# Slot weights of a mixture-of-experts layer: from one-hot matmuls to a gather from DRAM

## The chip, the cores and the metric

The kernel runs on one core of a Trainium2 chip. The metric is the device time of one execution in microseconds (us); lower is better. The core has a matrix engine (PE, with PEld for its weight loads), a vector engine (DVE), a scalar engine (ACT), GpSimd (POOL) and a sync engine (SP). Each engine takes its own instructions strictly in the order in which they were written for it; an instruction that waits holds up all that stand behind it on that engine. PE writes only into PSUM banks; DVE and ACT read them out. SP issues the loads of weights, POOL the indirect transfers (gather and scatter by row number).

## The reference, cut to what matters

One encoder layer on 512 tokens of width 1024: gated attention beside a spatial gating unit, a cross-attention, and a mixture of 16 experts, of which each token uses two. All inputs are float32. The part that the change is about:

```python
def hierarchical_moe(h, w_rg, b_rg, w_re, b_re, w_gate, w_up, w_down):
    t = h.reshape(B * S, D)                                   # 512 x 1024
    gprob = softmax(t @ w_rg + b_rg)                          # 4 groups
    gval, gidx = top_k(gprob, 1)
    elog_sel = (t @ w_re + b_re).reshape(-1, 4, 4)[group gidx]
    evals, eidx = top_k(elog_sel, 2)
    ew = softmax(evals) * gval
    expert_id = gidx * 4 + eidx
    combine = sum(one_hot(expert_id, 16) * ew[..., None])     # 512 x 16
    for e in range(16):
        he = silu(t @ w_gate[e]) * (t @ w_up[e])              # 1024 -> 512
        y = y + combine[:, e:e + 1] * (he @ w_down[e])        # 512 -> 1024
```

## The kernel before, in words

The first 455 us or so hold the attention parts and the router. Then 16 experts follow one another; that stage takes the rest of the span and is what the change touches.

**Slots.** For every expert the kernel gathers the tokens that chose it into 128 slots, so that one PE pass serves the expert. `oh_e(e)` builds on DVE a one-hot matrix (token by slot) from the positions `posm`. `ids_e(e)` multiplies it on PE with a small table `vals` (four matmuls, one for each 128 tokens), so that a PSUM bank holds, slot by slot, the row number of the token in `h3d` (the normed tokens in DRAM) and its row in the output buffer `ybuf`; DVE turns them into integers in `ixall`. `gather` is an indirect DMA from `h3d` into `xes[e % 2]`, `xtr` transposes that tile on PE (eight transposes into `pt_xt`, two banks) and splits it into a high and a low part.

**Slot weights, before.** `vals` has five columns: two for the numbers and three for the combine weight, cut into three float16 pieces by `weight_tables` on POOL (9 instructions for the weights, 8 more for the pieces). `slot_weights` puts the three pieces together on DVE in four small instructions (`sw`, then a column of `wsl`). For experts 0 to 3 (`NLATE`) the numbers are wanted before the weights are known; for these `late(e)` builds the one-hot again, runs `weight_of` (four more matmuls into a bank, `wt_e`, and the four DVE instructions), then scales the finished output `ye[e]` on ACT and scatters it. From expert 4 on, ACT scales while it reads the output out of PSUM.

**Weights of the experts.** Each expert has six chunks of 1 MB: 0 and 1 gate, 2 and 3 up, 4 and 5 down. A chunk is two halves. A half is split for fp32 accuracy: ACT rounds it into `h_e` (L128), DVE subtracts to get `l_e` (L129, a "low"). The fourth field of `W.order` names the halves whose low goes to POOL instead: in the experts 1 to 14, one of the twelve halves, the first of chunk 1 (`POOLJ`). PE runs six matmuls for each half: h with h, l with h, h with l (L237 to L239).

**Order.** `expert_period(e)` is one round: eight halves of gate and up of expert e, with a table `hooks[j, i]` of things to do after half i of chunk j, then `fin` (silu times up), `xtr` of expert e+1, and `down_scatter(e - 1)`, four halves of the expert before. After every half, `W.done` starts the conversion (ACT, then DVE or POOL) of a half further on. `h_e(e - 1)` at hook (0, 1) transposes the hidden tile into `pt_h`. In a round, `oh_e(e + 2)` stands at (0, 1), `ids_g(e + 2)` (numbers and gather) at (2, 1), and in rounds 2 to 5 `oh_e(e - 2)` at (1, 0) and `late(e - 2)` at (3, 0). `combine_weights` (six small DVE instructions) and `weight_tables` stand at (1, 1) of round 1. The tiles `ids`, `wt`, `pt_h` and `pt_xt` share the PSUM tag "T", which has two banks used in turn: PE may write a bank only when the tile that was in it two places earlier has been read out.

Of the kernel before, what the change touches and what calls it, by code (L numbers as in the profile page):

```python
# [8 lines left out]
F32 = mybir.dt.float32  # L9
# [33 lines left out]
def encoder(ctx, tc, x, mem, wf, we, wr, br, gv, gcol, gqk, rope, lngb, wsT, bs, out):  # L43
# [142 lines left out]
    def add_e(e, js):  # L186
        for j in js:
            cid[e, j] = len(W.order)
            W.order.append((we[e, j], f"e{e}_{j}", 4, int(j == POOLJ and 0 < e < NE - 1)))

# [743 lines left out]
    G.memset(ones, 1.0)  # L934
    vals = rt_([P, NT, NE, 5], "vals", F16)
    for t in range(NT):
        G.tensor_scalar(vals[:, t, :, 0:2], pid[:, :, None].to_broadcast([P, NE, 2]), t * P - BIGI, None, op0=ALU.add)
    lgt = rt_([P, NT, 20], "lgt")
    h3d = dr.tile([S, D], F32, name="h3d")
    ybuf = dr.tile([2 * S, D], F32, name="ybuf")  # L940
    zt = cr.tile([P, 512], F32, tag="zt", name="zt")
# [232 lines left out]

    wsl = rt_([P, NE], "wsl")
    WS = 1024.0
    WK = 2048.0
# [8 lines left out]
    def ids(name, oh, e, ix, n=2):  # L1186
        pi = bank("T", f"ids_{name}")
        for t in range(NT):
            T.matmul(pi[:, :n], oh[:, t], vals[:, t, e, 0:n], start=t == 0, stop=t == NT - 1)
        V.tensor_scalar(ix, pi[:, 0:2], BIGI, None, op0=ALU.add)  # L1190
        if n > 2:
            slot_weights(name, pi, e)
        return ix
# [34 lines left out]

    def ids_e(e, n=5):
        ixs[e] = ids(f"e{e}", ohs[e], e, ixall[:, e], n)  # L1230

    def weight_of(e):
        pi = bank("T", f"wt_e{e}")
        for t in range(NT):
            T.matmul(pi[:, 2:5], ohs[e][:, t], vals[:, t, e, 2:5], start=t == 0, stop=t == NT - 1)
        slot_weights(f"e{e}", pi, e)

# [89 lines left out]
    def down_scatter(e, pumps=(1, 1, 1, 1)):  # L1327
        if e == 0:
            yt = W.take("y12", [P, 2, D])
            ys.extend(yt[:, i] for i in range(2))  # L1330
        y = ye[e] = ys[e % len(ys)]
        sc = {} if e < NLATE else {"scale": wsl[:, e:e + 1]}
        down(e, lambda n, ps: A.activation(y[:, n * 512:(n + 1) * 512], ps, AF.Copy, **sc), pumps)  # L1333
        if e >= NLATE:
            y_scatter(e)

    def late(e):
        weight_of(e)
        A.activation(ye[e], ye[e], AF.Copy, scale=wsl[:, e:e + 1])
        y_scatter(e)  # L1340
# [6 lines left out]
    def expert_period(e):  # L1347
# [27 lines left out]
        if e == NE - 2:  # L1375
# [286 lines left out]
```

## Time and profile before

| | us |
|---|---|
| median of 3 runs (800.66 to 801.23) | 800.75 |
| the profiled execution, its own time | 801.04 |
| its span, first to last instruction | 799.2 |
| PE busy, of the span | 740.8 (93%) |
| DVE busy | 619.4 (78%) |
| ACT busy | 467.0 (58%) |
| POOL busy | 188.6 (24%) |

Busy time on PE is modelled from pipelined matmuls, so 93% does not mean that PE is at its peak; a wait shows as a gap between two instructions. Shares are means over very different stages: what counts here is the expert stage, in which PE, DVE and the DMA engines are all near full. The profile also lists the TensorE clock that was granted: 1.0 is 2.4 GHz, 0.5 is 1.2 GHz.

### The profile page before, as it was taken

What the parts mean: (1) busy time and instruction counts of PE and PEld (TensorE: products, weight loads), DVE (VectorE), ACT (ScalarE), POOL (GpSimd) and SP (SyncE); (2) the same over time, 40 slices, a digit from 0 to 9 for tenths busy, and PEclk for the clock granted to TensorE, in tenths of its full rate; (3) what the DMA queues carried; (4) which work ended last, traced back from release to release, by engine and by line L of the source; (5) the groups of instructions that cost most, each with busy time, mean ns of one, the idle gap of its engine ahead of it and who ended that gap; (6) DMA issues with size and microseconds to landing.
All of it is one profiled execution on the core that took longest, in us unless ns stands there. A gap on an engine that the chain in (4) does not pass through costs nothing.

```text
span 799.2 us, 10761 instructions
## 1 busy us (share of the span) xinstructions
PE 740.8 (93%) x3915; PEld 616.7 (77%) x3916; DVE 619.4 (78%) x1082; ACT 467.0 (58%) x711; POOL 188.6 (24%) x152
## 2 busy tenths in 40 slices
PE   4987999999999999999999997888999999999992
PEld 3775899778888888899988866666778888887781
DVE  5869899988562525568767789588989999999865
ACT  4545666665432322345555457566688888888753
POOL 4425312232000010102312037222132233332120
PEclk9999999999999999999999999899999999999996
DMA  7303121111222245346615289998789999999192
GB/s 283 131 5 154 54 106 53 55 53 53 81 78 105 106 145 206 128 164 247 235 66 207 110 341 420 391 340 310 299 287 385 361 382 367 373 375 355 53 204 109
DMA packets 28733, 163.42 MB, mean 204 GB/s; under 512 B 5071, under 2 KB 5103, under 8 KB 12416
## 3 DMA queue, kind: packets, MB, share of 16 engines
q1 hardware_dynamic: 19728, 137.90, 45.7%
q0 software_dynamic: 8224, 22.13, 8.8%
q10 hardware_dynamic: 720, 2.62, 0.8%
q8 instruction: 33, 0.54, 0.3%
q14 instruction: 28, 0.23, 0.1%
HBM read 154.63 MB, written 15.73 MB: 213 GB/s over the span
## 4 chain that ended last, share of the span: by engine, by line
PE 61%; DVE 22%; ACT 8%; issue 5%; DMA 3%; SPq 0%; DVEq 0%; ACTq 0%
DVE l_e L129 5%; PE g L237 3%; PE g L238 3%; PE g L239 3%; PE y_e L237 3%; PE y_e L239 3%; PE y_e L238 2%; PE g_e L239 2%; PE g_e L237 2%; PE u_e L237 2%; PE g_e L238 2%; PE u_e L239 2%; PE u_e L238 2%; DMA r_e<-in_we_dram 2%; ACT h_e L128 2%
## 5 line engine op out<-in xcount | busy, mean ns | idle before, releaser
L129 DVE TENSOR_TENSOR l_e<-r_e,h_e 128x1024 fp32r<-128x1024 f32 x174 | 225.2, 1337 | 28.2 <-ACT h_e L128 27.9
L128 ACT ACTIVATE h_e<-r_e 128x1024 fp32r<-128x1024 f32 x188 | 192.1, 1059 | 26.6 <-PE u_e L239 8.4
L238 PE MATMUL g_e<-l_e,xh_e 128*128 128x512 f32 x124 | 49.8, 402 | 7.1 <-POOL l_e L129 7.1
L237 PE MATMUL g_e<-h_e,xh_e 128*128 128x512 f32 x124 | 51.2, 413 | 0.9 <-ACT xh_e L231 0.9
L239 PE MATMUL g_e<-h_e,xl_e 128*128 128x512 f32 x124 | 49.9, 403 | 0.6 <-DVE xl_e L232 0.6
L237 PE MATMUL u_e<-h_e,xh_e 128*128 128x512 f32 x124 | 50.4, 407 | 0.0
L129 POOL TENSOR_TENSOR l_e<-r_e,h_e 128x1024 fp32r<-128x1024 f32 x14 | 37.7, 2693 | 53.3 <-ACT h_e L128 46.9
L237 PE MATMUL y_e<-h_e,hh_e 128*128 128x512 f32 x120 | 49.3, 411 | 0.8 <-ACT hh_e L231 0.8
L239 PE MATMUL u_e<-h_e,xl_e 128*128 128x512 f32 x124 | 49.0, 395 | 0.0
L238 PE MATMUL u_e<-l_e,xh_e 128*128 128x512 f32 x124 | 48.9, 394 | 0.0
L239 PE MATMUL y_e<-h_e,hl_e 128*128 128x512 f32 x120 | 48.1, 401 | 0.0
L238 PE MATMUL y_e<-l_e,hh_e 128*128 128x512 f32 x120 | 47.8, 399 | 0.0
L1196 POOL DMA_INDIRECT xe<-h3d,ixall x15 | 16.4, 1096 | 130.4 <-DVE sw_e L1183 111.4
L580 ACT ACTIVATE p<-s,nm,qsc 128x512 f32<-128x512 f32 x32 | 25.1, 783 | 35.6 <-DVE nm L577 20.5
L238 PEld LDWEIGHTS g_e<-l_e,xh_e 128*128 128x128 f32 x124 | 23.9, 193 | 12.3 <-POOL l_e L129 7.4
L239 PEld LDWEIGHTS g_e<-h_e,xl_e 128*128 128x128 f32 x124 | 23.8, 192 | 7.0 <-DVE xl_e L232 1.5
L237 PEld LDWEIGHTS g_e<-h_e,xh_e 128*128 128x128 f32 x124 | 23.8, 192 | 6.1 <-ACT xh_e L231 1.4
L1218 POOL DMA_INDIRECT ybuf<-y,ixall x14 | 21.1, 1509 | 27.5 <-ACT y L1333 15.7
L239 PEld LDWEIGHTS u_e<-h_e,xl_e 128*128 128x128 f32 x124 | 23.3, 188 | 5.5
L237 PEld LDWEIGHTS y_e<-h_e,hh_e 128*128 128x128 f32 x120 | 23.0, 192 | 5.7 <-ACT hh_e L231 1.1
L239 PEld LDWEIGHTS y_e<-h_e,hl_e 128*128 128x128 f32 x120 | 22.9, 191 | 5.8 <-DVE hl_e L232 0.4
L129 DVE TENSOR_TENSOR l_wo<-r_wo,h_wo 128x1024 fp32r<-128x1024 f32 x8 | 9.8, 1226 | 22.6 <-ACT h_wo L128 22.6
(453 smaller groups left out, 2192.0 us busy)
## 6 DMA issues: line engine op xcount, KB each, us to landing
r_e<-in_we_dram SPq DMA_DIRECT2D x96, 1024.0 KB, 7.7
r_a<-in_wf_dram SPq DMA_DIRECT2D x4, 1024.0 KB, 5.0
r_b<-in_wf_dram SPq DMA_DIRECT2D x4, 1024.0 KB, 4.8
r_y<-in_wf_dram SPq DMA_DIRECT2D x4, 1024.0 KB, 4.7
r_wo<-in_wf_dram SPq DMA_DIRECT2D x4, 1024.0 KB, 4.8
ybuf<-zt POOLq DMA_DIRECT2D x2, 2048.0 KB, 13.6
xr<-ybuf POOLq DMA_DIRECT2D x8, 512.0 KB, 9.7
xt<-in_x_dram SPq DMA_DIRECT2D x4, 512.0 KB, 7.8
```

Source lines behind the costliest of these rows:

```text
L128: A.activation(h, rr, AF.Copy)
L129: lo = lambda X=G if onpool >> i & 1 else V, l=l, rr=rr, h=h: X.tensor_tensor(l, rr, h, op=ALU.subtract)
L237: T.matmul(ps, ah, bh, start=first and i == 0, stop=False)
L238: T.matmul(ps, ah, bl, start=False, stop=False)
L239: T.matmul(ps, al, bh, start=False, stop=last and i == n - 1)
L580: A.activation(pr, ps, AF.Exp, bias=nm, scale=qsc[t][:, h:h + 1], accum_out=sx)
L1196: G.indirect_dma_start(out=xe, out_offset=None, in_=h3d, in_offset=bass.IndirectOffsetOnAxis(ap=ix[:, 0:1], axis=0), bounds_check=S - 1, o ...
L1218: return G.indirect_dma_start(out=ybuf, out_offset=bass.IndirectOffsetOnAxis(ap=ix[:, 1:2], axis=0), in_=y, in_offset=None, bounds_check=2 ...
```

## The change

Slot weights are no longer computed with the one-hot. `weight_tables` makes the 512 x 16 table of combine weights (9 POOL instructions) and writes it to DRAM as `cwd`. `gather_w(e)` gathers for each slot the row of 16 weights (64 bytes) by the same row numbers, with one indirect DMA on POOL's queue, into one of eight rows of `cwg`; `wof(e)` is the column of expert e in it, which ACT uses as the scale. `vals` keeps two columns. `slot_weights`, `weight_of`, `wsl` and the eight POOL instructions for the pieces are gone.

The numbers are found four experts ahead (`AHEAD`): `oh_e(e + 4)` at (0, 0), `ids_e(e + 4)` at (1, 1); round 1 does those of experts 4 and 5 besides. The gather of the tokens is taken out of the hook: it stands after `xtr` at the end of a round and is for expert e+3, followed from round 3 on by `gather_w(e + 3)`. `combine_weights` and `weight_tables` move from (1, 1) of round 1 to (3, 0) and (3, 1) of round 2; the weights of experts 0 to 5 are gathered in round 3 at (1, 1) and (3, 0). Only experts 0 to 2 are late (`NLATE` 3): they are scaled and scattered in round 4 at (0, 1) and (3, 0) and in round 5 at (2, 0). No low of an expert's half goes to POOL any more.

```diff
-POOLJ = 1
+AHEAD = 4
+NCW = 8
-NLATE = 4
+NLATE = 3
...
-            W.order.append((we[e, j], f"e{e}_{j}", 4, int(j == POOLJ and 0 < e < NE - 1)))
+            W.order.append((we[e, j], f"e{e}_{j}", 4, 0))
...
-    vals = rt_([P, NT, NE, 5], "vals", F16)
+    vals = rt_([P, NT, NE, 2], "vals", F16)
...
+    cwd = dr.tile([S, NE], F32, name="cwd")
...
-    def slot_weights(name, pi, e):
-        sw = sm.tile([P, 3], F32, tag="sw", bufs=2, name=f"sw_{name}")
-        V.tensor_copy(sw, pi[:, 2:5])
-        for i in (1, 0):
-            V.scalar_tensor_tensor(sw[:, i:i + 1], sw[:, i + 1:i + 2], 1.0 / WK, sw[:, i:i + 1], op0=ALU.mult, op1=ALU.add)
-        V.tensor_scalar(wsl[:, e:e + 1], sw[:, 0:1], 1.0 / WS, None, op0=ALU.mult)
...
+    cwg = rt_([P, NCW, NE], "cwg")
+    G.memset(cwg, 0.0)
+
+    def wof(e):
+        return cwg[:, e % NCW, e:e + 1]
+
+    def gather_w(e):
+        G.indirect_dma_start(out=cwg[:, e % NCW], out_offset=None, in_=cwd,
+                             in_offset=bass.IndirectOffsetOnAxis(ap=ixs[e][:, 0:1], axis=0),
+                             bounds_check=S - 1, oob_is_err=False)
...
         G.tensor_tensor(cw, cw, cb, op=ALU.add)
-        G.tensor_scalar(cb, cw, WS, None, op0=ALU.mult)
-        for i in range(3):
-            G.tensor_copy(vals[:, :, :, 2 + i], cb)
-            if i < 2:
-                G.tensor_tensor(cb, cb, vals[:, :, :, 2 + i], op=ALU.subtract)
-                G.tensor_scalar(cb, cb, WK, None, op0=ALU.mult)
+        G.dma_start(cwd.rearrange("(t p) e -> p t e", p=P), cw)
...
         elif e == 1:
-            hooks[0, 0] += [lambda: ids_g(3, 2)]
-            hooks[1, 0] += [lambda: ids_e(0, 2)]
-            hooks[1, 1] += [combine_weights, weight_tables]
-        elif e + 2 < NE:
-            hooks[0, 1].append(lambda: oh_e(e + 2))
-            hooks[2, 1].append(lambda: ids_g(e + 2))
-        if 2 <= e < 2 + NLATE:
-            hooks[1, 0].append(lambda: oh_e(e - 2))
-            hooks[3, 0].append(lambda: late(e - 2))
+            hooks[0, 0] += [lambda: ids_g(3)]
+            hooks[0, 1] += [lambda: oh_e(4)]
+            hooks[1, 0] += [lambda: ids_e(0)]
+            hooks[1, 1] += [lambda: ids_e(4), lambda: oh_e(5)]
+            hooks[2, 1] += [lambda: ids_e(5)]
+        elif e + AHEAD < NE:
+            hooks[0, 0].append(lambda: oh_e(e + AHEAD))
+            hooks[1, 1].append(lambda: ids_e(e + AHEAD))
+        if e == 2:
+            hooks[3, 0].append(combine_weights)
+            hooks[3, 1].append(weight_tables)
+        elif e == 3:
+            hooks[1, 1].append(lambda: [gather_w(n) for n in range(3)])
+            hooks[3, 0].append(lambda: [gather_w(n) for n in range(3, 6)])
+        late_at = {4: {(0, 1): 0, (3, 0): 1}, 5: {(2, 0): 2}}
...
         if e:
             xT[e + 1] = xtr(f"e{e + 1}", xes[(e + 1) % 2])
+        if 0 < e < NE - 3:
+            gather(ixs[e + 3], xes[(e + 1) % 2])
+            if e > 2:
+                gather_w(e + 3)
```

How the order of instructions moves is shown at two places. The number behind a tile's name tells one use of it from the next; line numbers are those of each kernel. First DVE, in the second half of round 3, before: `l_e_3` is a low of chunk 3, `oh_e` here the repeated one-hot for a late expert, `g` is `fin`.

```order
L129 TENSOR_TENSOR l_e_3_5213<-r_e_3_4738,h_e_3_5212 128x1024
L1171 TENSOR_TENSOR oh_e_5218<-io_3529,posm 128x512
L129 TENSOR_TENSOR l_e_4_5227<-r_e_4_4819,h_e_4_5226 128x1024
L129 TENSOR_TENSOR l_e_4_5237<-r_e_4_4819,h_e_4_5236 128x1024
L129 TENSOR_TENSOR l_e_5_5251<-r_e_5_4871,h_e_5_5250 128x1024
L1190 TENSOR_SCALAR ixall<-ids_e_5254 128x2
L1181 COPY sw_e_5260<-ids_e_5254 128x3
L1183 SCALAR_TENSOR_TENSOR sw_e_5260<-sw_e_5260 128x1 x2
L1184 TENSOR_SCALAR wsl<-sw_e_5260 128x1
L129 TENSOR_TENSOR l_e_5_5275<-r_e_5_4871,h_e_5_5274 128x1024
L1181 COPY sw_e_5285<-wt_e_5280 128x3
```

Between two lows stand the read-out of the numbers (`ixall`), then that of their three weight pieces, and a low later the second read-out, that of `wt`; the changed kernel has this instead, at the same place of DVE in the same round:

```order
L130 TENSOR_TENSOR l_e_3_5206<-r_e_3_4740,h_e_3_5205 128x1024
L130 TENSOR_TENSOR l_e_4_5218<-r_e_4_4823,h_e_4_5217 128x1024
L1181 TENSOR_SCALAR ixall<-ids_e_5221 128x2
L130 TENSOR_TENSOR l_e_4_5243<-r_e_4_4823,h_e_4_5242 128x1024
L130 TENSOR_TENSOR l_e_5_5257<-r_e_5_4859,h_e_5_5256 128x1024
L130 TENSOR_TENSOR l_e_5_5267<-r_e_5_4859,h_e_5_5266 128x1024
L130 TENSOR_TENSOR l_e_0_5288<-r_e_0_4889,h_e_0_5287 128x1024
L1290 TENSOR_TENSOR g_5248<-g_5248,u_e_5165 128x512
```

The read-out of the numbers stands two lows earlier, and the read-outs of the weight pieces and the repeated one-hot are gone.

Second POOL, from the tables of weights on, before (`hi` and `vals` are the pieces, `l_e_1` the low of chunk 1 of expert 2):

```order
L1281 TENSOR_TENSOR hi_4113<-hi_4113,vals 128x64
L1282 TENSOR_SCALAR hi_4113<-hi_4113 128x64
L1279 CAST vals<-hi_4113 128x64
L129 TENSOR_TENSOR l_e_1_4946<-r_e_1_4636,h_e_1_4945 128x1024
L1196 DMA xe_4519<-h3d,ixall 128x1024
L1218 DMA ybuf<-y_4645,ixall 1024x1024
```

The low is queued behind all of the tables; this is POOL at the same place, from the table's last instruction on, in the changed kernel:

```order
L1270 TENSOR_TENSOR lgt<-lgt,hi_4114 128x4x16
L1271 DMA cwd<-lgt 128x4x16
L1185 DMA xe_4521<-h3d,ixall 128x1024
L1228 DMA cwg<-cwd,ixall 128x16 x6
L1185 DMA xe_4520<-h3d,ixall 128x1024
L1228 DMA cwg<-cwd,ixall 128x16
L1207 DMA ybuf<-y_4647,ixall 1024x1024
```

No low stands behind the tables; the write of the table, the gather of tokens of expert 5 and the first six gathers of weights follow it.

## Rows read from the trace of the kernel before

**Rows 1.** Cores: span and mean granted TensorE clock.
```profile
core 0: 799.2 us, clock 0.977
```

**Rows 2.** Windows: busy us (x count) PE PEld DVE ACT POOL; clock; DMA; GB/s.
```profile
460.00:500.00 40.00, 33.28 (x163) 25.83 (x161) 34.62 (x49) 25.73 (x32) 22.81 (x22) 0.99 0.94 385
500.00:540.00 40.00, 35.26 (x165) 27.64 (x166) 28.14 (x43) 25.18 (x31) 9.22 (x6) 0.92 0.93 363
540.00:580.00 40.00, 35.55 (x169) 27.46 (x168) 35.50 (x49) 27.62 (x33) 8.42 (x5) 0.96 0.83 306
...
620.00:660.00 40.00, 40.00 (x191) 32.13 (x190) 38.47 (x46) 33.51 (x40) 12.40 (x7) 1.00 0.98 372
```

**Rows 3.** Timeline of PE: start, duration; where rounds 1, 7 and 13 end.
```profile
484.95 0.38 PE L296 MATMUL pt_xt_e<-identf,xe 128*128 128x128 f32 x2
...
615.91 0.49 PE L296 MATMUL pt_xt_e<-identf,xe 128*128 128x128 f32 x3
...
726.42 0.49 PE L296 MATMUL pt_xt_e<-identf,xe 128*128 128x128 f32 x3
```

**Rows 4.** Waits from 460 to 600 us: total us, times, longest.
```profile
ACT y L1339 <- DVE wsl L1184: 19.4, 4, 6.3
...
PE g_e L238 <- POOL l_e L129: 7.1, 1, 7.1
...
PE pt_xt_e L296 <- DVE sw_e L1181: 4.5, 4, 1.1
```

**Rows 5.** Timeline of POOL, rounds 1 and 2.
```profile
482.91 3.64 POOL L1274 TENSOR_SCALAR lgt<-io,i,gval 128x16 f32<-128x16 f32 x1 [3.70 <-DVE gval L1269]
...
491.24 0.32 POOL L1276 TENSOR_TENSOR lgt<-lgt,hi 128x64 f32<-128x64 f32 x1
...
499.30 2.77 POOL L129 TENSOR_TENSOR l_e<-r_e,h_e 128x1024 fp32r<-128x1024 f32 x1
```

**Rows 6.** Timeline of PE at chunk 1 of expert 2.
```profile
494.54 0.48 PE L237 MATMUL g_e<-h_e,xh_e 128*128 128x512 f32 x1
...
502.13 0.79 PE L238 MATMUL g_e<-l_e,xh_e 128*128 128x512 f32 x1 [7.11 <-POOL l_e L129]
```

**Rows 7.** Timeline of PE and DVE at the end of round 4.
```profile
549.50 0.26 PE L1189 MATMUL ids_e<-vals,oh_e 128*128 128x5 f16 x4
...
554.50 0.15 DVE L1181 COPY sw_e<-ids_e 128x3 f32<-128x3 f32 x1
...
554.75 0.63 PE L296 MATMUL pt_xt_e<-identf,xe 128*128 128x128 f32 x4 [1.85 <-issue]
...
555.15 1.22 DVE L129 TENSOR_TENSOR l_e<-r_e,h_e 128x1024 fp32r<-128x1024 f32 x1
556.28 0.15 DVE L1181 COPY sw_e<-wt_e 128x3 f32<-128x3 f32 x1
...
556.49 0.66 PE L296 MATMUL pt_xt_e<-identf,xe 128*128 128x128 f32 x4 [1.11 <-DVE sw_e L1181]
```

**Rows 8.** Timeline: lows on DVE alone, a low on POOL, one on DVE beside it.
```profile
629.98 4.62 DVE L129 TENSOR_TENSOR l_e<-r_e,h_e 128x1024 fp32r<-128x1024 f32 x4
...
640.13 2.66 POOL L129 TENSOR_TENSOR l_e<-r_e,h_e 128x1024 fp32r<-128x1024 f32 x1 [4.16 <-ACT h_e L128]
...
640.97 2.91 DVE L129 TENSOR_TENSOR l_e<-r_e,h_e 128x1024 fp32r<-128x1024 f32 x1 [0.45 <-ACT h_e L128]
```

**Rows 9.** Timeline: issues of a gather and a scatter on POOL, lows on DVE beside them.
```profile
616.53 1.02 POOL L1196 DMA_INDIRECT xe<-h3d,ixall  x1 [8.61 <-DVE sw_e L1183]
...
616.83 2.35 DVE L129 TENSOR_TENSOR l_e<-r_e,h_e 128x1024 fp32r<-128x1024 f32 x2
...
640.97 6.31 DVE L129 TENSOR_TENSOR l_e<-r_e,h_e 128x1024 fp32r<-128x1024 f32 x4 [0.45 <-ACT h_e L128]
...
642.95 1.79 POOL L1218 DMA_INDIRECT ybuf<-y,ixall  x1 [0.16 <-ACT h_e L128]
```

**Rows 10.** Indirect transfers by `ixall`: issue to landing.
```profile
DMA to landing us min/median/max: 3.2/8.5/11.0
```

More of the change, by code (lines that the diff above doesn't have):

```diff
@@ L934, in encoder @@
     G.memset(ones, 1.0)
-    vals = rt_([P, NT, NE, 5], "vals", F16)
+    vals = rt_([P, NT, NE, 2], "vals", F16)
     for t in range(NT):
-        G.tensor_scalar(vals[:, t, :, 0:2], pid[:, :, None].to_broadcast([P, NE, 2]), t * P - BIGI, None, op0=ALU.add)
+        G.tensor_scalar(vals[:, t], pid[:, :, None].to_broadcast([P, NE, 2]), t * P - BIGI, None, op0=ALU.add)
     lgt = rt_([P, NT, 20], "lgt")
     h3d = dr.tile([S, D], F32, name="h3d")
+    cwd = dr.tile([S, NE], F32, name="cwd")
     ybuf = dr.tile([2 * S, D], F32, name="ybuf")
@@ L1173, in onehot, with ids @@
         return oh
-    wsl = rt_([P, NE], "wsl")
-    WS = 1024.0
-    WK = 2048.0
-    def slot_weights(name, pi, e):
-        sw = sm.tile([P, 3], F32, tag="sw", bufs=2, name=f"sw_{name}")
-        V.tensor_copy(sw, pi[:, 2:5])
-        for i in (1, 0):
-            V.scalar_tensor_tensor(sw[:, i:i + 1], sw[:, i + 1:i + 2], 1.0 / WK, sw[:, i:i + 1], op0=ALU.mult, op1=ALU.add)
-        V.tensor_scalar(wsl[:, e:e + 1], sw[:, 0:1], 1.0 / WS, None, op0=ALU.mult)
-    def ids(name, oh, e, ix, n=2):
+    def ids(name, oh, e, ix):
         pi = bank("T", f"ids_{name}")
         for t in range(NT):
-            T.matmul(pi[:, :n], oh[:, t], vals[:, t, e, 0:n], start=t == 0, stop=t == NT - 1)
+            T.matmul(pi[:, :2], oh[:, t], vals[:, t, e], start=t == 0, stop=t == NT - 1)
         V.tensor_scalar(ix, pi[:, 0:2], BIGI, None, op0=ALU.add)
-        if n > 2:
-            slot_weights(name, pi, e)
         return ix
@@ L1227, in oh_e, with ids_e @@
         ohs[e] = onehot(f"e{e}", posm[:, :, e])
[L1229 to L1236, printed above, removed]
+    def ids_e(e):
+        ixs[e] = ids(f"e{e}", ohs[e], e, ixall[:, e])
+    cwg = rt_([P, NCW, NE], "cwg")
[6 more added lines that the diff above has]
+                             bounds_check=S - 1, oob_is_err=False)
     raw4 = ctx.enter_context(pool("raw4", side=L))
@@ L1245, in encoder @@
     xT[0] = xh0, xl0
-    ids_e(1, 2)
+    ids_e(1)
     gather(ixs[1], xes[1])
@@ L1331, in down_scatter @@
         y = ye[e] = ys[e % len(ys)]
-        sc = {} if e < NLATE else {"scale": wsl[:, e:e + 1]}
+        sc = {} if e < NLATE else {"scale": wof(e)}
         down(e, lambda n, ps: A.activation(y[:, n * 512:(n + 1) * 512], ps, AF.Copy, **sc), pumps)
@@ L1337, in late @@
     def late(e):
-        weight_of(e)
-        A.activation(ye[e], ye[e], AF.Copy, scale=wsl[:, e:e + 1])
+        A.activation(ye[e], ye[e], AF.Copy, scale=wof(e))
         y_scatter(e)
@@ L1353, in expert_period, with ids_g @@
         hooks[2, 0] = [lambda: mid(e)]
-        def ids_g(n, k=5):
-            ids_e(n, k)
+        def ids_g(n):
+            ids_e(n)
             gather(ixs[n], xes[n % 2])
@@ L1361, in expert_period @@
             hooks[2, 0] += [counts]
-            hooks[2, 1] = [lambda: ids_g(2, 2), lambda: oh_e(3)]
+            hooks[2, 1] = [lambda: ids_g(2), lambda: oh_e(3)]
             hooks[3, 0] = [lambda: xT.update({1: xtr("e1", xes[1], xslot)})]
@@ L1365, in expert_period @@
         elif e == 1:
-            hooks[0, 0] += [lambda: ids_g(3, 2)]
-            hooks[1, 0] += [lambda: ids_e(0, 2)]
-            hooks[1, 1] += [combine_weights, weight_tables]
-        elif e + 2 < NE:
-            hooks[0, 1].append(lambda: oh_e(e + 2))
-            hooks[2, 1].append(lambda: ids_g(e + 2))
-        if 2 <= e < 2 + NLATE:
-            hooks[1, 0].append(lambda: oh_e(e - 2))
-            hooks[3, 0].append(lambda: late(e - 2))
+            hooks[0, 0] += [lambda: ids_g(3)]
[13 more added lines that the diff above has]
+        late_at = {4: {(0, 1): 0, (3, 0): 1}, 5: {(2, 0): 2}}
+        for at_, n in late_at.get(e, {}).items():
+            hooks[at_].append(lambda n=n: late(n))
         if e == NE - 2:
@@ L1404, in evac @@
     def evac(i):
-        w = wsl[:, NE - 2 + i:NE - 1 + i]
+        w = wof(NE - 2 + i)
         yhl[i] = W.spare(f"yhl{i}", [P, 2, D], F32R)
```

## The prediction

> **What bounds the kernel now.** The cores view first: one core, 799.2 us of span [rows 1]. The profiled execution took 801.04 us, so 1.84 us lie outside the span, and it stands 0.29 us above the median of 800.75. The sum below is made on the span, and these two are put in at its end.
>
> The windows by stage come next [rows 2]. A row gives the stretch and its length, then the busy time of each engine. From 620 us on PE is busy all 40.00 of 40 us at full clock. From 460 to 580 us it lacks 6.7, 4.7 and 4.5 us, and the clock falls to 0.92 and 0.96. So the expert stage has a smooth part, which PE sets, and a rough part ahead of it. The timeline of PE gives the size of the roughness, if the same instruction is looked up in each round, the first transpose of the next expert's tokens [rows 3]. From round 7 to round 13 that is 726.42 - 615.91 = 110.51 us for six rounds, 18.42 us for one. From round 1 to round 7, also six, it is 130.96 us. **20.45 us** more: that is all that a change of order can win here, as long as the 18.42 stay, since a round has the same 72 large matmuls with or without the change.
>
> Where it goes is read from the waits [rows 4] and then from the timeline around each. There are two kinds.
>
> *One long stop in round 2.* PE has the high part of expert 2's chunk 1 at 494.54 and gets its low only at 502.13: 7.11 us idle on POOL [rows 4, 6]. POOL had begun the tables of weights at 482.91 and ended them just before the low, which ran at 499.30 for 2.77 us [rows 5]. So the low was no slow instruction: it stood 16.4 us behind work that nobody needed yet. The window after it has a mean clock of 0.92 [rows 2]: for a part of it the granted clock was at 1.2 GHz instead of 2.4. A mean lower by 0.08 over 40 us is 3.2 us of lost pulses, some of them while PE was idle anyway; I put it at about 2 us, an estimate. Together about 9.
>
> *Stops at the ends of rounds 3 to 6.* In round 4 PE does the numbers' matmuls at 549.50, and a half later those of the weights of a late expert. Then the eight transposes need the two "T" banks. The first four begin at 554.75, right after DVE's copy out of the first bank at 554.50; the others at 556.49, after the copy out of the second at 556.28 [rows 7]. PE is idle 1.85 and 1.11 us, because DVE takes its queue in order and has lows ahead of the copies. The copies wait 4 times for 4.5 us in the waits [rows 4]; with the part ascribed to issue and the slow clock after the longest stop (0.96 [rows 2]), the rest of the 20.45, about 11 us, belongs to these round ends.
>
> **The change, part by part.**
>
> *The low of chunk 1 goes to DVE.* In round 2 it then stands on DVE right behind the lows of chunk 0, ahead of those of chunk 2, and not behind the tables; DVE had over 5 of 40 us free around there [rows 2]. The 9 us of the long stop go. What does DVE pay for it, in every round? A low costs 4.62 / 4 = 1.16 us there. But while POOL works on its low, DVE stands still: the low begun at 640.97 took 2.91 us, 1.70 more than the 1.21 of one by itself, and POOL's ended at 642.79, 1.82 us after DVE's began [rows 8]. So DVE gets 1.70 back for 1.16.
>
> *The weight read-outs go.* From the copy at 554.50 to the next low at 555.15 they cost 0.65 us of DVE a round [rows 7], twice that in the rounds with a late expert, which also lose a one-hot. DVE was busy 38.47 of 40 us in the smooth part [rows 2], 17.7 us of a round. After: 17.7 + 1.16 - 1.70 - 0.65 = **16.5 us** of 18.42. It stays below PE.
>
> *The numbers are read earlier.* Their matmuls move from (2, 1) to (1, 1), four halves, some 5.6 us (an estimate: a half is about 1.4 us, a twelfth of 18.42 less the transposes). In round 4 the first copy came about 5.0 us after its matmuls [rows 7]. Moved 5.6 us ahead and with no second bank (`wt`) behind it, even a DVE that lags as much as now has freed the bank before the transposes. The 11 us go as well. What is late next: the matmuls of the numbers need the one-hot, now at (0, 0), three halves ahead, 4.2 us. Ahead of it DVE has two or three lows, some 3 us; it fits, with about 1 us of room.
>
> *New work.* On PE nothing in a round: four matmuls for the numbers as before, without the four of the late experts. Round 1 has two groups of them more (0.26 us each [rows 7]), rounds 12 and 13 one less. In round 0 the read-out of expert 2's numbers, which the transposes wait for, now stands behind a low that POOL did: up to 1.16 us, once. The bounds of all of these are 0 and 1.7; I take 0.7, since the groups are given back.
>
> POOL gets a gather of weights a round; a gather's issue takes 1.02 us [rows 9], and POOL loses a low of 2.66 [rows 8]. Behind the two gathers in its queue stands only the scatter, which goes out after four more halves of PE, 5.6 us. The landing is wanted no sooner than a round later, from expert 3 on. The token gathers are moved too: they wait on POOL for the transposes that read their tile, and are wanted two rounds later, 37 us against a landing of 11 [rows 10] at the most: nothing.
>
> *A new wait.* ACT's scaling of the late expert 0 in round 4 now hangs on: the tables (482.91 to 491.56, 8.6 us [rows 5]), the write of the table to DRAM, one gather that waits for it on POOL, and ACT in order behind it. Rounds of 18.42 us from 484.95 put the start of the tables at about 505.5, the end at 514. No row shows 64-byte pieces; landings of the indirect transfers are 3.2 to 11.0 us, median 8.5 [rows 10]. Two of them and 1.02 us for the issue give 521.5 to 537, by the median 532. ACT reaches the place at about 533. So the wait is 0 to 4 us; I take 0, since those transfers move 4 KB a row and these 64 bytes, and keep 4 for the range: behind ACT's scaling stand all the conversions. The Trainium skill (DMA: Bandwidth & Descriptors, Anatomy of one DMA) puts a small transfer at about 2 us, nearly all of it fixed; by it, an estimate, the weights lie there at about 519 (514, 2, 1, 2), the sum stays, and the rival of late weights below has no chance. No run shows such a transfer yet, so it keeps one.
>
> The sum: 799.2 - 20.45 + 0.7 = 779.45 of span; + 1.84 = 781.3 for such an execution; - 0.29 = **781.0 us** as a median.
>
> **The rivals.**
>
> *Late weights.* ACT waits up to 4 us once: 781.0 + 4 = 785. For: the medians leave 1 us. Against: the pieces are small.
>
> *Weight loads set the pace.* The smooth rounds move 372 GB/s at a DMA share of 0.98 [rows 2], and the rough ones would now want the same. The unhindered loading ran at 385 and 363. If 363 is the limit, five rounds take 2.5% longer, 2.3 us: 783.3. Against: DMA share was only 0.83 in 540 to 580 us, so the loads were ahead.
>
> *The round ends stay.* If DVE's queue does not get shorter (it has one more low) or PE now waits for the one-hot, the 11 us stay and only the long stop goes: 781.0 + 11 = 792.
>
> *Slower: POOL's issues lock DVE.* A round now has three indirect issues: two of about 1.02 and a scatter of 1.79 [rows 9], 3.8 us. If each stopped DVE as POOL's low does, DVE would need 16.5 + 3.8 = 20.3 us, and PE would follow: 13 rounds of 1.9 us more give 781.0 + 25 = 806. It turns slower than before when more than 20 us / 13 = 1.5 us a round is lost beyond 18.42, so with 3.4 of the 3.8 us locked. For it: the low on POOL locked 1.70 of 1.82 us. Against it: two lows beside a gather took 2.35 us, as on their own; and of the 6.31 us of four lows [rows 9] the first took 2.91 [rows 8], so the other three, beside the scatter, 1.1 to 1.2 each. The Trainium skill (SBUF — State Buffer, Who interferes with whom) has the rule behind this rival: the two engines share a port pair that one of them holds for a whole instruction, while the other fully blocks. For the low the trace agrees; for the issues it does not, and the page itself infers that writing descriptors needs another part of the pair than such lows take.
>
> **How the numbers follow.** Chances: forecast 0.72, late weights 0.10, weight loads 0.05, round ends 0.08, slower 0.05. The predicted time is the forecast's, 781.0. The range takes in the first three, 0.87: from 778, if the new costs are 0 and the short stops of round 1 (not counted above) shrink too, up to 789, where a wait of 4 us, the loads' 2.3 and part of the round ends fall together. Faster by over 0.2% (1.6 us, about what a measurement of this kernel can tell from no change) is all but the last: 0.94; slower 0.05; the same 0.01, for round ends that grow by just what the long stop gives.
>
> **What would show it.** In the profile after: no wait of PE on a low in round 2 and a clock of 1.00 from 500 to 580 us; first transposes 18.4 us apart from round 1 on; no transpose waiting for a copy; lows on DVE of 1.2 us without any of 2.9; DVE idle 1.5 to 2 us a round. Wrong would be: PE waiting at the numbers for `oh_e`, ACT waiting for `cwg` in round 4, or lows of over 1.4 us beside gathers.

## The result, and the profile after

The changed kernel takes **776.39 us** as a median of 4 runs (774.42 to 779.66), beside 800.99 for the kernel before in the same set: a ratio of 0.9695, with a 95% interval of 0.966 to 0.973. The prediction was 781.0 us with a range of 778 to 789. The side was right; the gain is 24.6 us where 20 were forecast, and the median lies 1.6 us under the range.

The profiled execution took 774.42 us, with a span of 772.7. First the windows by stage, to be held against [rows 2] (busy time and count of PE, PEld, DVE, ACT, POOL; granted clock; DMA share; GB/s):

```profile
500.00:540.00 40.00, 40.00 (x200) 32.85 (x199) 38.38 (x47) 34.61 (x43) 25.26 (x22) 1.00 1.02 415
540.00:580.00 40.00, 39.53 (x192) 32.21 (x191) 36.48 (x40) 32.99 (x40) 16.88 (x9) 1.00 1.01 399
620.00:660.00 40.00, 40.00 (x200) 32.65 (x199) 37.65 (x42) 34.42 (x41) 7.19 (x6) 1.00 1.00 385
```

The rough part is gone: from 500 us on PE is busy all but 0.47 of 80 us at full clock, where it lacked 9.2. The loads kept up (415 GB/s against 363), so the rival of the weight loads falls. Next the transposes that end a round, as in [rows 3]: here the ends of rounds 0, 1, 7, 11 and 14.

```profile
466.55 0.60 PE L297 MATMUL pt_xt_e<-identf,xe 128*128 128x128 f32 x4
468.26 0.66 PE L297 MATMUL pt_xt_e<-identf,xe 128*128 128x128 f32 x4 [1.11 <-DVE ixall L1181]
...
483.90 1.03 PE L297 MATMUL pt_xt_e<-identf,xe 128*128 128x128 f32 x8
...
592.68 1.04 PE L297 MATMUL pt_xt_e<-identf,xe 128*128 128x128 f32 x8
...
664.83 1.03 PE L297 MATMUL pt_xt_e<-identf,xe 128*128 128x128 f32 x8
...
718.58 1.03 PE L297 MATMUL pt_xt_e<-identf,xe 128*128 128x128 f32 x8
```

A round's length is taken from one end's first transpose to the next. Rounds 2 to 7 take 108.78 us where they took 130.96: 22.18 less, more than the 20.45 that the prediction called all that could be won. And the smooth rounds are shorter too: from the end of round 7 to that of round 11 it is 72.15 / 4 = **18.04 us** a round. The same in the kernel before, at the ends of rounds 0, 7, 11 and 14:

```profile
468.39 1.04 PE L296 MATMUL pt_xt_e<-identf,xe 128*128 128x128 f32 x8
...
615.91 1.20 PE L296 MATMUL pt_xt_e<-identf,xe 128*128 128x128 f32 x8
...
689.61 1.18 PE L296 MATMUL pt_xt_e<-identf,xe 128*128 128x128 f32 x8
...
744.95 1.03 PE L296 MATMUL pt_xt_e<-identf,xe 128*128 128x128 f32 x8
```

That is 73.70 / 4 = 18.43. With these rows the whole difference of the two spans, 26.5 us, can be set out against the forecast:

| part of the span | forecast, us less | measured |
|---|---|---|
| up to the end of round 0 | 0 | 1.84 |
| round 1 (more numbers, one low more) | -0.7 | -0.79 |
| rounds 2 to 7 | 20.45 | 22.18 |
| rounds 8 to 14 | 0 | 3.14 |
| after round 14 | 0 | 0.13 |

The first 1.84 us are no work of the change. Ahead of the experts the granted clock falls to 1.2 GHz for a stretch in some executions and not in others: from 440 to 460 us its mean is 1.00 in this profile, 0.91 in that of before, and 0.83 in a second profile of the changed kernel, whose span is 777.6 us. That profile is 4.9 us longer than the first: 2.9 lie ahead of the end of round 0 and 2.0 in round 5. So the spread of 5 us among its runs has at least these two sources. What has to be explained is the shorter smooth round: 13 rounds of 0.39 us.

The waits of PE from 460 to 740 us (total, times, longest) show what is left:

```profile
PE pt_xt_e L297 <- DVE ixall L1181: 1.1, 1, 1.1
PE y_e L238 <- ACT hh_e L232: 0.8, 1, 0.8
PE g_e L240 <- DVE xl_e L233: 0.5, 1, 0.5
PE ids_e L1180 <- DVE oh_e L1173: 0.5, 1, 0.5
```

No low, no copy of a weight piece [rows 4]. The last row is a stop in round 5, 550.04 to 550.90, which the experiments take up at the end.

### The profile page after: what moved, and what is told of

Read it like the earlier page. It is cut to its first block, busy times and chain, and to the rows that moved or that the text cites. A ratio compares the mean times of both kernels' runs of the same rounds, so it can differ in the third digit from the quotient of the medians.

```text
span 772.7 us, 10679 instructions
## 1 busy us (share of the span) xinstructions
PE 728.5 (94%) x3899; PEld 611.4 (79%) x3900; DVE 602.9 (78%) x1028; ACT 466.3 (60%) x710; POOL 169.6 (22%) x148
## 4 chain that ended last, share of the span: by engine, by line
PE 71%; DVE 15%; ACT 7%; DMA 3%; issue 3%; SPq 0%; ACTq 0%; DVEq 0%; POOLq 0%
PE u_e L238 4%; PE y_e L238 4%; PE y_e L240 4%; PE y_e L239 3%; PE u_e L240 3%; PE u_e L239 3%; PE g_e L238 3%; PE g_e L240 3%; PE g_e L239 3%; PE g L238 3%; PE g L239 3%; PE g L240 3%; PE y L239 2%; PE y L240 2%; PE y L238 2%
## 5 line engine op out<-in xcount | busy, mean ns | idle before, releaser
L130 DVE TENSOR_TENSOR l_e<-r_e,h_e 128x1024 fp32r<-128x1024 f32 x188 | 221.2, 1218 | 20.8 <-ACT h_e L129 20.4
L129 ACT ACTIVATE h_e<-r_e 128x1024 fp32r<-128x1024 f32 x188 | 191.3, 1055 | 16.5 <-PE u_e L240 7.9
L1185 POOL DMA_INDIRECT xe<-h3d,ixall x15 | 18.9, 1263 | 108.8 <-PE pt_xt_e L297 72.3
L239 PEld LDWEIGHTS u_e<-l_e,xh_e 128*128 128x128 f32 x124 | 23.3, 188 | 4.5
L238 PEld LDWEIGHTS u_e<-h_e,xh_e 128*128 128x128 f32 x124 | 23.3, 188 | 4.5
```

The costliest lines, as they stand in the source:

```text
L129: A.activation(h, rr, AF.Copy)
L130: lo = lambda X=G if onpool >> i & 1 else V, l=l, rr=rr, h=h: X.tensor_tensor(l, rr, h, op=ALU.subtract)
L238: T.matmul(ps, ah, bh, start=first and i == 0, stop=False)
L239: T.matmul(ps, ah, bl, start=False, stop=False)
L1185: G.indirect_dma_start(out=xe, out_offset=None, in_=h3d, in_offset=bass.IndirectOffsetOnAxis(ap=ix[:, 0:1], axis=0), bounds_check=S - 1, o ...
```

## The experiments

Twelve kernels ran on the chip, eight of them to find where 0.39 us a round come from. Times are medians; they come from four sets of runs, and each ratio is to the kernel before in the same set. The smooth round is taken from the transposes at the ends of rounds 7 and 11 of each profile.

| kernel | us | ratio, 95% | smooth round |
|---|---|---|---|
| before (one in each set) | 801.57, 801.72, 800.81, 800.78 | 1 | 18.43 |
| before, no low on POOL | 788.73 | 0.9818 to 0.9865 | 18.26 |
| before, `sw` behind the weight tiles | 802.81 | 0.9995 to 1.0022 | 18.43 |
| before, both of these | 786.81 | 0.9797 to 0.9845 | 18.05 |
| changed, again | 777.24 | 0.9658 to 0.9711 | 18.04 |
| changed, low of chunk 1 on POOL | 784.78 | 0.9773 to 0.9811 | 18.04 |
| changed, 64 bytes of padding | 779.20 | 0.9704 to 0.9745 | 18.24 |
| changed, `xh`, `xl`, `hh`, `hl` 64 bytes down | 779.77 | 0.9692 to 0.9743 | 18.24 |
| changed, numbers at the old place | 778.81 | 0.9688 to 0.9734 | 18.04 |
| changed, tables earlier | 776.41 | 0.9668 to 0.9715 | 18.04 |
| changed, 192 bytes of padding | 774.10 | 0.9634 to 0.9685 | 17.97 |
| the same, tables earlier | 774.69 | 0.9647 to 0.9686 | 17.97 |
| 192 bytes, gathers of weights later | 772.61 | 0.9638 to 0.9664 | 17.97 |

### The changed kernel again

No edit.

> The changed kernel once more, unchanged. Its smooth rounds took 18.03 us where those of the kernel before took 18.42, which no step of the prediction gave. Four theories. RUN: the pace belongs to the single execution; then the smooth round here is another number between 18.0 and 18.4. LOW: a low on POOL slows the matmuls of its round. PLACE: without the tile sw all weight tiles lie 64 bytes lower, and the pace follows the addresses. ORDER: the pace follows what stands between the groups of large matmuls. By the last three the round is 18.03 again (spacing of large matmuls 229 ns), and the time 774 to 780.

It took 777.24 us (774.52 to 779.47), with the same 18.04 us a round, and each of the rounds 1 to 14 within 0.03 us of its twin in the first profile, but for round 5. The pace belongs to the program, not to the execution: RUN falls.

### One part undone: a low on POOL again

```diff
-            W.order.append((we[e, j], f"e{e}_{j}", 4, 0))
+            W.order.append((we[e, j], f"e{e}_{j}", 4, int(j == 1 and 0 < e < NE - 1)))
```

> The changed kernel with one part undone: in the experts 1 to 14 the low of the first half of chunk 1 goes to POOL again. The prediction's step on the long stop: that low of expert 3 now stands on POOL behind the tables (to 514.7 us), the write of the table and a gather, so it ends at about 519 and PE wants it at about 511: a stop of 8 us in round 3, 10 with a slow clock behind it, while the other rounds have none. The lock: lows on DVE beside it take 2.9 us, others 1.2. Pace: LOW expects smooth rounds of about 18.3 (spacing 232), so 776 + 10 + 2.5 = 789; PLACE and ORDER 18.03, so 786.

784.78 us, 7.5 more than without. The long stop is back, one round later, since the tables are. PE at chunk 1 of expert 3, and POOL (start, duration, engine, line, what; idle before):

```profile
512.38 0.48 PE L238 MATMUL g_e<-h_e,xh_e 128*128 128x512 f32 x1
519.25 0.79 PE L239 MATMUL g_e<-l_e,xh_e 128*128 128x512 f32 x1 [6.39 <-POOL l_e L130]
```

```profile
513.62 0.56 POOL L1270 TENSOR_TENSOR lgt<-lgt,hi 128x64 f32<-128x64 f32 x1
514.48 0.89 POOL L1271 DMA_DIRECT2D cwd<-lgt  x1 [0.30 <-POOL lgt L1270]
515.68 1.08 POOL L1185 DMA_INDIRECT xe<-h3d,ixall  x1 [0.31 <-issue]
516.78 2.42 POOL L130 TENSOR_TENSOR l_e<-r_e,h_e 128x1024 fp32r<-128x1024 f32 x1
```

Round 3 takes 26.63 us, 8.6 more than its neighbours: 6.39 of waiting and about 2 beside a mean clock of 0.91 from 520 to 540 us, as the prediction put it for round 2 (7.11 and 2). So the step on the long stop holds, and its cure is the low that left POOL, not the place of the tables. But the smooth rounds are 18.04 as without: LOW falls. The lock is back as well: the longest low on DVE is 3.36 us, against 1.28 in the changed kernel. So a low on POOL costs DVE time in each round here, and PE none, as DVE has time to spare.

### One part alone: no low on POOL in the kernel before

```diff
-            W.order.append((we[e, j], f"e{e}_{j}", 4, int(j == POOLJ and 0 < e < NE - 1)))
+            W.order.append((we[e, j], f"e{e}_{j}", 4, 0))
```

> The kernel before with one part alone: no low goes to POOL. The prediction's step: the long stop of round 2 goes, 7.11 us and about 2 for the slow clock, while the transposes at the ends of rounds 3 to 6 still wait for the copies of the weight pieces (1.1 to 1.9 us each). 801 - 9 = 792 by PLACE, ORDER and RUN, with smooth rounds of 18.42; by LOW the smooth round falls to about 18.15 and the time to 789. If the lock of DVE was what made the round ends late, they go too: 781.

788.73 us: half of the gain for one field of a table. Round 2 falls from 27.72 to 20.81 us, not to 18.3, because the next thing that needs the tables now waits for them, the numbers' matmuls, which read all five columns of `vals`:

```profile
503.06 0.24 PE L1189 MATMUL ids_e<-vals,oh_e 128*128 128x5 f16 x4 [2.20 <-POOL vals L1279]
```

Rounds 4 and 5 are still 2.6 us longer than its smooth ones, with transposes that wait for the copies. Rounds 2 to 7 together take 119.5 us, 10.0 above six of its own smooth rounds: of the 20.45 us, the low on POOL was the cause of about half. Of the 10.0, 2.6 are the new wait of round 2, and 7.4 lie in rounds 3 to 7, which in the kernel before are 11.1 above its smooth ones. So 3.7 us of the round ends went with the low too, as the last sentence of the expectation has it, and two thirds of them stayed. The smooth round is 18.26, between the two kernels: 0.17 of the 0.39 us came with the low, and the next runs are for the other 0.22.

### The weight tiles at their old addresses

A tile of 64 bytes a partition, in a pool ahead of the weight tiles:

```diff
+    pad = const.tile([P, 16], F32, name="pad")
+    nc.gpsimd.memset(pad, 0.0)
```

> The changed kernel with an unused tile of 64 bytes a partition ahead of the weight tiles, so that these lie at the addresses that they had in the kernel before. PLACE expects the old pace: smooth rounds of about 18.3 us, 232 ns from matmul to matmul, 780 us. LOW and ORDER expect no change: 18.03 and 776.

779.20 us, and a round of 18.24:

```profile
595.18 1.03 PE L299 MATMUL pt_xt_e<-identf,xe 128*128 128x128 f32 x8
...
668.14 1.03 PE L299 MATMUL pt_xt_e<-identf,xe 128*128 128x128 f32 x8
```

PLACE holds, and it accounts for the rest of the 0.39. The two buffers of `sw` take 64 bytes of a partition, ahead of all weight tiles; the change drops `sw`, so `h` and `l` lie 64 bytes lower. The 24 matmuls of the downs take 5.65 to 5.68 us, from the first one's start to the start of what follows, with the padding and in the smooth rounds of the kernel before, 5.57 to 5.60 without it. The first step of the 24 is 0.31 to 0.32 us in all of them; the others are 232 and 229 ns from matmul to matmul. Nothing waits in either; the instructions are the same ones in the same order.

### The place alone, in the kernel before

```diff
-        sw = sm.tile([P, 3], F32, tag="sw", bufs=2, name=f"sw_{name}")
+        sw = mx.tile([P, 3], F32, tag="sw", bufs=2, name=f"sw_{name}")
```

> The kernel before with one part alone: the small tile sw lies behind the weight tiles instead of ahead of them, so the tiles h and l lie 64 bytes lower, as in the changed kernel; no instruction is added, dropped or moved. PLACE, by the run with 64 bytes of padding (smooth rounds of 18.24 us for 18.03): spacing of large matmuls 229 ns instead of 232, a smooth round of 18.42 - 0.21 = 18.2 and 13 x 0.21 = 2.7 us less in all, 798 to 799. Against it (the pace comes with the new order and the padding disturbed something else): 18.42 and no difference.

A miss: 802.81 us, no difference (0.9995 to 1.0022), and rounds of 18.43. Yet its matmuls are the quick ones, 5.57 to 5.59 us for 24. What they win is lost at the round's end (PE):

```profile
652.33 0.60 PE L296 MATMUL pt_xt_e<-identf,xe 128*128 128x128 f32 x4
653.12 0.63 PE L296 MATMUL pt_xt_e<-identf,xe 128*128 128x128 f32 x4 [0.20 <-DVE sw_e L1181]
```

The second four transposes wait for the copy of the weight pieces, so that the eight take 1.42 us and not 1.03. In the kernel before they take 1.20 and 1.18 (615.91 and 689.61 above): there too PE waits a little in every smooth round. Its waits from 616 to 740 us show that only as a weight load of the transposes that waits for nothing the profile sees:

```profile
PEld pt_xt_e L296 <- issue: 1.0, 6, 0.2
```

In six rounds that is 1.0 us, 0.17 a round, just what the round becomes shorter without the low on POOL (18.43 to 18.26). What it waits for is a loop over DVE (DVE and POOL, one round of the kernel with `sw` moved):

```profile
653.48 2.35 DVE L129 TENSOR_TENSOR l_e<-r_e,h_e 128x1024 fp32r<-128x1024 f32 x2
655.74 0.68 DVE L1301 TENSOR_TENSOR g<-g,u_e 128x512 f32<-128x512 f32 x1
656.34 1.28 DVE L232 TENSOR_TENSOR xl_e<-pt_xt_e,xh_e 128x512 fp32r<-128x512 f32 x2
657.54 1.22 DVE L129 TENSOR_TENSOR l_e<-r_e,h_e 128x1024 fp32r<-128x1024 f32 x1
659.17 6.36 DVE L129 TENSOR_TENSOR l_e<-r_e,h_e 128x1024 fp32r<-128x1024 f32 x4 [0.41 <-ACT h_e L128]
665.45 0.68 DVE L232 TENSOR_TENSOR hl_e<-pt_h_e,hh_e 128x512 fp32r<-128x512 f32 x1
666.05 0.68 DVE L1171 TENSOR_TENSOR oh_e<-io,posm 128x512 f16<-128x512 bf16 x1
666.65 4.62 DVE L129 TENSOR_TENSOR l_e<-r_e,h_e 128x1024 fp32r<-128x1024 f32 x4
671.19 0.15 DVE L1190 TENSOR_SCALAR ixall<-ids_e 128x2 int32<-128x2 f32 x1
```

```profile
658.33 2.72 POOL L129 TENSOR_TENSOR l_e<-r_e,h_e 128x1024 fp32r<-128x1024 f32 x1 [4.13 <-ACT h_e L128]
```

The transposes wait for the copy that follows `ixall`; the downs follow the transposes; ACT reads the downs' first output and then rounds the next halves; DVE's low at 659.17 waits for one of these; and from there to the copy DVE has work without a gap, 1.7 us of it the stop beside POOL's low. So the kernel before ran its smooth rounds at DVE's pace, 18.43 us, whatever PE could do.

### Both parts in the kernel before

Both diffs above together.

> The kernel before with two parts: the tile sw behind the weight tiles, and no low on POOL. The first alone gave nothing: its matmuls were quicker (229 ns), but the transposes waited longer for DVE, and the round stayed at 18.43 us; the second alone gave rounds of 18.25. If DVE with its stops beside POOL's low is what sets 18.42, and PE by itself needs 18.25 at the old distance of the operands and 18.03 at the new one, both together give 18.03, and 788.7 - 13 x 0.22 = 786. If the two gains are not of that kind, 18.25 and 788.7.

The smooth round is 18.05: each gain shows once the other obstacle is gone. The time is 786.81 us, 1.9 less than without the lower addresses where 2.9 were expected; round 2 took 22.27 us instead of 20.81, since the numbers wait longer for the tables.

### Which address counts

`xh`, `xl`, `hh` and `hl`, which PE loads as weights, 64 bytes lower, by a tile of that size in a pool beside theirs; `h` and `l`, which stream, stay:

```diff
+    mp = ctx.enter_context(pool("mopad", side=R))
+    pad = mp.tile([P, 16], F32, name="pad")
+    G.memset(pad, 0.0)
     mo = ctx.enter_context(pool("moe", bufs=2, side=R))
```

> The changed kernel with the tiles xh, xl, hh and hl (the operand that PE loads as weights) moved 64 bytes down, and h and l (the operand that streams) left where they are. DISTANCE: what counts is how far the two operands of a matmul lie apart; that is again the distance of the kernel before (128 bytes, modulo 512, instead of 192), so the slow pace: 18.24 us a round, 779. ADDRESS: what counts is where h and l lie; then 18.03 and 777.

18.24 us a round and 779.77: the slow pace, as with the padding, to 0.01 us in each of the rounds 6 to 14. DISTANCE holds. In the built programs, modulo 512, `xh` lies at 480 in both kernels, `h` at 352 before and at 288 after the change. To move `h` up or `xh` down by 64 is the same to the matmuls.

### A better distance

```diff
-NCW = 8
+NCW = 7
...
+    pad = const.tile([P, 48], F32, name="pad")
+    nc.gpsimd.memset(pad, 0.0)
```

> The changed kernel with 192 bytes of padding ahead of the weight tiles (and seven rows of weights in cwg instead of eight, for room), so that h and l lie at the same place as xh and xl modulo 512. In round 1, where xh has such a place already, the spacing of the last matmuls is 226.7 ns in both kernels. DISTANCE: 226.7 instead of 228.7 everywhere, 72 x 2 ns = 0.14 us less a round: 17.89, and 775. ADDRESS: no telling, between 17.9 and 18.3.

A round of 17.97, half of the 0.14 that was expected, and 774.10 us. Of the 3.1 us to the changed kernel's second median, 13 rounds of 0.07 explain 0.9; the rest is within what its runs spread. The direction holds (the 24 matmuls of the downs take 5.54 to 5.56 us); other distances were not tried.

### The numbers at their old place

```diff
-            hooks[0, 0].append(lambda: oh_e(e + AHEAD))
-            hooks[1, 1].append(lambda: ids_e(e + AHEAD))
+            hooks[0, 1].append(lambda: oh_e(e + AHEAD))
+            hooks[2, 1].append(lambda: ids_e(e + AHEAD))
```

> The changed kernel with one part undone: from round 2 on the one-hot stands at (0, 1) and the matmuls of the numbers at (2, 1) again, as before. The prediction's step (the 11 us of the round ends go because the numbers are read four halves earlier) expects the transposes to wait for the copy again, the more the longer DVE's queue: up to 1.3 us a round in rounds 3 to 6, some 3 to 5 us in all, 780. The rival: the repeated one-hots and the second bank of the late experts were the cause, and the place of the numbers is indifferent: 18.03 a round, 777, and the wait for the one-hot in round 5 (0.5 to 0.6 us) goes.

The rival is right, but for one round. Rounds 2 to 4 and 7 to 11 are as long as in the changed kernel, and no transpose waits there. Only at the end of round 5 one does, 1.06 us for `ixall`, since DVE is late in that round as it is in the changed kernel; the wait for the one-hot stays too (0.4). In all 778.81 against 777.24 us, a difference within what the runs of the changed kernel spread. So it is not the early numbers that free the round ends. What is left as their cause, beside the low on POOL with its 3.7 us, is the second one-hot, the second bank and the read-outs of the weights; these three were not taken apart. That the numbers are read four halves earlier is worth a microsecond or so, at one place.

### What makes round 5 late: the tables earlier

```diff
-            hooks[3, 0].append(combine_weights)
-            hooks[3, 1].append(weight_tables)
+            hooks[1, 0].append(combine_weights)
+            hooks[1, 1].append(weight_tables)
```

> The changed kernel with combine_weights and weight_tables two chunks earlier, at (1, 0) and (1, 1) of round 2. It is for the one stop that is left in its expert stage, between the transposes at 537.93 and 556.61, which are 0.64 us farther apart than the others (2.6 in the second run). CHAIN: tables until 514.7, their write until 521, six gathers of weights on POOL until 529, so the scatter of the late expert 0 goes out at 533.5, 2 us after ACT has scaled it, and lands at about 543.4; ACT wants its tile for the next output at 541.6 and waits 2 us, and the conversions and the one-hot behind it come late. Then here the scatter goes out at 531.8, ACT waits 0 to 0.5 us and the interval is 18.0. OTHER: the stop comes from the scaling itself or from DVE's queue; then 18.5 or more. Time 776 either way, less 0.6 to 1.5 by CHAIN.

776.41 us and the long interval still 18.68: nothing gained, and CHAIN neither shown nor refuted, since the scatter did not go out earlier. POOL began the first gather of weights 3.6 us earlier and lost that again, beside a train of four lows on DVE:

```profile
518.07 5.42 POOL L1228 DMA_INDIRECT cwg<-cwd,ixall  x1 [3.72 <-DMA cwd<-lgt]
523.79 1.01 POOL L1228 DMA_INDIRECT cwg<-cwd,ixall  x1 [0.30 <-issue]
...
534.33 1.28 POOL L1207 DMA_INDIRECT ybuf<-y,ixall  x1 [0.30 <-issue]
```

```profile
517.99 4.62 DVE L130 TENSOR_TENSOR l_e<-r_e,h_e 128x1024 fp32r<-128x1024 f32 x4
```

With the 192 bytes as well:

> The changed kernel with 192 bytes of padding ahead of the weight tiles (seven rows in cwg) and the tables at (1, 0) and (1, 1) of round 2: the run with 192 bytes took 774.1 with rounds of 17.97 and one of 18.73; without that one 773.3.

774.69 us, no different from the padding alone; the long interval is 18.75.

### The scatter ahead of the gathers

With 192 bytes of padding, and:

```diff
-            hooks[3, 0].append(lambda: [gather_w(n) for n in range(3, 6)])
+        elif e == 4:
+            hooks[1, 0].append(lambda: [gather_w(n) for n in range(3, 6)])
```

> The changed kernel with 192 bytes of padding (rounds of 17.97 us, one of 18.73, 774.1 in its run), and the gathers of the weights of experts 3 to 5 moved behind the scatter of the late expert 0, to (1, 0) of round 4. Moving the tables did not bring that scatter out earlier: it went out 10.2 us ahead of ACT's late read-out, as before, because POOL had lost 4.4 us elsewhere. Here three issues of about 1.3 us stand behind the scatter and no longer ahead of it. CHAIN (ACT waits for the landing of that scatter, whose tile it wants to write): the scatter goes out right behind ACT's scaling, about 2 us earlier, ACT's wait of 3.1 us falls to 1.1 to 1.5 as at the other round ends, and the long interval is 17.97 like the others: 0.75 us less. OTHER (the scaling itself, or DVE): the interval stays at 18.7 and the time at 774 to 775.

**772.61 us** (772.28 to 773.13), a ratio of 0.9638 to 0.9664 to the kernel before: the lowest median, 3.8 us under the changed kernel's first (the rounds explain 0.9 of it, the long interval 0.6). Its ratio overlaps that of the padding alone, so the step is read from the interval and not from the time. CHAIN holds. In the changed kernel the scatter of expert 0 and ACT's first read-out of expert 3, which takes over its tile, are:

```profile
533.51 1.28 POOL L1207 DMA_INDIRECT ybuf<-y,ixall  x1 [0.30 <-ACT h_e L129]
```

```profile
543.74 0.69 ACT L1322 ACTIVATE y<-y_e,cwg 128x512 f32<-128x512 f32 x1 [3.14 <-PE y_e L239]
```

and here:

```profile
531.24 1.32 POOL L1209 DMA_INDIRECT ybuf<-y,ixall  x1 [2.99 <-ACT y L1329]
```

```profile
541.24 0.69 ACT L1324 ACTIVATE y<-y_e,cwg 128x512 f32<-128x512 f32 x1 [1.14 <-PE y_e L242]
```

The wait of 3.14 us is put down to PE, but PE had ended these matmuls some 2 us before. The trace has the scatter land 10.2 us after its issue, so at 543.7, when ACT goes on; in the six other profiles in which ACT waits there for over 3 us, the read-out follows the scatter by 10.1 to 10.6 us. It is the transfer's landing. (In the run with `xh` moved, POOL happened to be free, the scatter went out at once, ACT waited 1.19 us and round 5 was as long as the others.) With the scatter 2.3 us earlier, landed at 540.0, the wait is 1.14, as at any round end, the conversions behind it are in time, and the long interval is 17.96.

## Why the prediction was wrong, point by point

**The long stop: right.** Nothing of [rows 6] is left. Its price, 7.11 and about 2 for the clock, agrees with the run with the low on POOL again: 6.39 and about 2.

**The round ends: right in size, half wrong in reason.** Rounds 3 to 7 were 11.1 us longer than smooth ones; of that, 0.64 is left, in round 5. The prediction put the early numbers first and the missing second bank beside them. The run with the numbers at their old place shows that the early place is only a reserve for one late round. When nothing but the low was taken off POOL, 7.4 us stayed; so 3.7 went with that low, to which the prediction had charged the long stop only. The rest went with the second one-hot, the second bank and the read-outs of the weights, by elimination and not one by one.

**The step that failed: "as long as the 18.42 stay, since a round has the same 72 large matmuls".** It took from [rows 2] that PE sets the smooth part, because PE is busy 40.00 of 40 us. It does not: that round was DVE's. Busy time on PE hides short waits. The sign was there in the same timeline, the eight transposes that last 1.2 us in the smooth rounds and 1.03 at the ends of the first and the last. Freed of DVE, the round is 18.26 (no low on POOL); with the two operands 64 bytes farther apart, which came with the dropped tile `sw`, 18.04. These 0.17 and 0.22 us, 13 times, are 5.1 us, and the median lies 4.6 under the forecast. The first part could have been read from the trace; of the second nothing in the diff or the profile before speaks, unless one compares addresses.

**DVE's own account** was near: 16.5 us a round were forecast, 37.65 of 40 us, in the window from 620 us, are 17.0 of 18.04. None of its lows is slow any more: in the expert stage the longest is 1.28 us, where it was 3.21 (line, engine, shapes, count, busy us, mean ns, idle before):

```profile
L130 DVE TENSOR_TENSOR l_e<-r_e,h_e 128x1024 fp32r<-128x1024 f32 x188 | 221.2, 1218 | 20.8 <-ACT h_e L129 20.4
```

**New work: right in size.** Round 1 is 0.79 us longer. At the end of round 0 the transposes wait 1.11 us for `ixall`, as named; but that is not the price, since the kernel before without the low on POOL has the same wait (1.10) and a round 1 of 16.56 us, as long as with it. Rounds 12 and 13, without numbers, are 0.2 us shorter each.

**Late weights: did not happen, but a neighbour did.** ACT scales expert 0 at 530.31 us without waiting for `cwg`. The tables ended at 514.4, by the forecast at 514, and that is luck: they began at 503.35, 2 us earlier than forecast, and took 11.0 us for 8.6, as two of their POOL instructions took 3.48 and 2.90 us beside lows, where most of the others took 0.41 to 0.42. Their write landed 6.3 us after its issue and the gathers of weights 5.5 to 10.7 after theirs, inside the 3.2 to 11.0 of [rows 10] that were used. The 2 us that the Trainium skill (DMA: Bandwidth & Descriptors, Anatomy of one DMA) gives for a small transfer are not what these took, under a DMA share of 1.02; the measurement decides. The wait that did come, 0.64 us in this profile and 2.6 in the second, was a link farther on: the same crowded queue of POOL held the scatter of the late output, and ACT needed its tile. The prediction had looked at who waits for the weights and not at who waits for the tile.

**POOL's issues lock DVE: refuted, and the other way round.** No low is longer beside an issue. But the issues are, beside lows. POOL and DVE in round 5 of the changed kernel:

```profile
554.87 5.44 POOL L1207 DMA_INDIRECT ybuf<-y,ixall  x1 [6.21 <-DVE l_e L130]
```

```profile
554.84 4.62 DVE L130 TENSOR_TENSOR l_e<-r_e,h_e 128x1024 fp32r<-128x1024 f32 x4
```

That issue, of a scatter, takes 1.0 to 1.5 us elsewhere in this profile; here it begins 0.03 us after the start of a train of four lows and ends 0.9 us after the end of that train. In the run with the tables earlier, the first gather of weights did the same (5.42 us). The rule of the Trainium skill (SBUF — State Buffer, Who interferes with whom), one holder at a time, agrees with these two. The page's inference that the prediction quotes, that writing descriptors needs another part of the port pair than such lows take, does not agree with them. Nor is the wait a rule of these runs: with the numbers at their old place, an issue that began 0.05 us after a train of four took 2.04 us, and in the kernel before without the low on POOL one in the middle of six lows took 0.99. What decides is open. In the changed kernel the long issue held up nothing that a round's length shows; with the tables earlier it cost what they had gained.

**The signs.** Of the signs of being wrong that the prediction named, one came: PE waited for `oh_e`, once, 0.47 us in round 5.

## What to carry to other kernels

A stage in which an engine is "busy 40 of 40 us" may still run at another engine's pace: look in the timeline for one small instruction that lasts longer in these rounds than elsewhere, and follow it once round the loop before calling a round's length fixed. Of two obstacles on one loop, one can look worthless when it alone is removed (18.43 us before and after) and pay once the other is gone (18.26 to 18.05), so test them together before dropping either. When a scratch tile is added or dropped, the operands of the matmuls move; compare their addresses, and try a padding of a few times 64 bytes. After a change that empties one engine's queue, ask for each buffer that it recycles who waits for its last transfer.

## What the hardware showed that was not expected

The spacing of 512-column matmuls at full clock, fp32r from SBUF, follows how far the loaded and the streamed operand lie apart: 232 ns with `h` 128 bytes below `xh` modulo 512, 229 with 192, and 228 at the same place, where the round is 0.07 us shorter again. In two kernels with different addresses and one distance (64 bytes up for one operand, 64 down for the other) the smooth rounds agree to 0.01 us. That the modulus is 512 was not tested, nor was any reason; the Trainium skill (SBUF — State Buffer, Who interferes with whom) lists two read ports for PE, one for each operand, as independent, and these runs do not say where the two meet.
